# Splitting convolution weights during the seven products, norming the last result by pairs, and moving one stored piece of attention work

## The chip, the cores and the metric

The kernel runs on one core of one Trainium2 chip. Its metric is the device time of one execution in microseconds. Five engines work side by side, each through its own instruction stream in order: PE (TensorE, matrix products), DVE (VectorE), ACT (ScalarE), POOL (GpSimd) and SP (SyncE, which here only issues transfers). ACT also issues transfers, from inside its own stream. An instruction whose inputs or buffers aren't ready blocks everything behind it on its engine.

## The reference, cut to what matters

Two layers on 1024 tokens of width 1024 (all in float32): a windowed grouped-query attention layer, then a Conformer convolution layer, and a last RMSNorm.

```python
proj = h_lat @ w_in                                   # attention layer: q, k, v, z
o = windowed_attention(q, k, v, kc, vc, sink)         # 16 query heads, 4 kv heads, head width 128
y = (o * jax.nn.silu(z)) @ w_out                      # 2048 -> 1024
x = x + gate * y
h = modulate(rmsnorm(x, norm_g[1]), shift, scale)     # convolution layer
a, gl, z = jnp.split(h @ w_in + b_in, 3, axis=-1)     # 1024 -> 3 * 2048
u = a * jax.nn.sigmoid(gl)
u = depthwise_conv_31(u) + dw_b
u = jax.nn.silu(layernorm(u, ln_g, ln_b))
x = x + gate * ((u * jax.nn.silu(z)) @ w_out)         # 2048 -> 1024
return rmsnorm(x, final_g)
```

`depthwise_conv_31` stands for the reference's 31-tap convolution of every channel for itself.

## The kernel before, in words

**Products in float32.** TensorE multiplies in a shorter type, so a float32 operand is *split*: ACT copies it to a rounded high part, and another engine subtracts to get the low part. A product is then three matmuls (high·high, low·high, high·low). For the convolution weights the raw tile is `wraw`, the parts are `whi` (ACT) and `wlo` (DVE or POOL). For the attention output they are `ozf`, `ozh`, `ozl`, and for its weights `wo`, `woh`, `wol`. For the layer's input they are `h2h` (ACT) and `h2l` (DVE), with a helper tile `hf` (ACT) between them.

**Stages in order of time.**

1. Start, modulation vectors, first projections.
2. Attention: 128 steps, `(pr, st)`, a pair of heads and a block of 64 queries each. In a step PE computes scores (`pss`), DVE and ACT make the probabilities, POOL scales them by the row's reciprocal sum (`p_page <- p_page, sc`), and PE transposes them (`pss <- ident, p_page`). Between these PE fills its time with the projection of the next head's weights (`psg`), whose rotary turn is shared by ACT, two transfers issued from ACT's stream, DVE and POOL (`rope_half`), and whose query split is `qh` (ACT) and `ql` (POOL). POOL also prepares sums, differences and low parts of the two output weights in small pieces and stores them in device memory: `low_parts`, a generator of which the step loop takes one piece per step at most, and two in some steps (`wb`, `low`, `lhi`).
3. The attention's output projection by *seven products* in place of eight (`proj_attn`, list `SEQA`): `r = 0` with 8 `kk`, `r = 1..5` with 4 `kk`, each `(r, kk)` 24 matmuls 512 columns wide. The tiles of the next entries are loaded and split ahead by `ahead`. What `split` leaves for DVE (`ozl`) waits in a list until `flush()` is called. `bgA(r, kk)` is called after each entry, for background work. The last three entries (`r = 5`, `kk = 1..3`) are run row block by row block, `b = 0..3`: each block's sum is added to x (`first_sum`, `evac0`), its squares are summed on ACT (`junk`), and `norm0` turns them into a normed row block `xn`. `turn_in` transposes one of eight parts of the normed result on PE into a bank `pso` (two banks take turns) and makes `h2h`, `hf`, `h2l` from it; a bank is free again once `h2l` is made.
4. The convolution layer's input projection: 48 weight tiles (`border`), two halves of the tokens each (`b_mm(i, half)`), 24 matmuls for each. The first `FIRST = 5` tiles run half 0 one after the other, then half 1. Half 1's input is the last result of stage 3, so its eight `turn_in` calls stand inside `b_mm(2..4, 0)` (table `TURNS`), while half 0 only needs earlier results. Behind PE, ACT, DVE and POOL gate (`sig`, `ubuf`) and convolve (`prod`, `odd`, DVE's sums in `pss`).
5. Output projection of the convolution layer, last norm, store.

**What sets the order.** The kernel records operations in the order of the program text, and a planning layer, with a model of the engines, places them into each engine's stream. `tc.high_priority()` moves an operation forward in it, and `after(op, anchor)` ties it behind another one. For `WStream` with `hp=True`, that is the convolution weights, `whi` is made at high priority but tied behind `anchor_n`, the last `xn` written by ACT. Buffers come from two pools: `pg`, 45 pages of 1024 words, and `hp`, 6 half pages of 528. So when a buffer comes free sets when a load may be issued, and SP issues loads strictly in its order.

**Lines touched.** `rstd_one` (one row block's reciprocal root) and its caller `norm0`; `WStream.split`; `proj_attn` around `ahead(*LOAD_TO[i])`, `ahead(10, 9)` and the last block loop; `turn_in`; the step loop's `next(lows, "shut")`; the line that makes `wsB`; `bgA`; the loop over `FIRST`. All engine operations are recorded through one helper, so the profile shows one line number (L94, L96 in the changed kernel) for all of them, and tiles are told apart by name.

## Time and profile before

| | |
|---|---|
| Times of three runs | 1688.74, 1689.21, 1691.45 us, median 1689.21 |
| Profiled execution | 1689.08 us, span 1687.3 us from first to last instruction |
| Mean granted TensorE clock | 0.992 |
| Busy: PE, DVE, ACT, POOL | 1650.8 (98%), 1138.4 (67%), 899.7 (53%), 931.5 (55%) us |
| Start, 0 to 80 us | PE busy 77.0 of 80 us |
| Attention, 80 to 805 us | PE busy 719.8 of 725 us, POOL 457.2 |
| Seven products, 805 to 953 us | PE busy 143.9 of 148 us |
| First convolution tiles, 953 to 1003 us | PE busy 33.6 of 50 us, clock 0.83 |
| Rest of the input projection, 1003 to 1502 us | PE busy 499.0 of 499 us, DVE 473.3, POOL 398.2 |
| Output projection, 1502 to 1679 us | PE busy 177.0 of 177 us |
| Tail | 8.3 us |

How to read it: PE is busy for nearly the whole span, so a change can save time only where PE stands still or its clock is lowered, and it costs time wherever another engine becomes late for PE. The stage table shows where PE stands still. The trace numbers all times from the first instruction of the span.

### The profile page before, as it was taken

The numbers are of one execution on the slowest core, as the hardware profiler recorded it, in microseconds if no ns is written. First come the engines' busy times: TensorE is split into PE (matmuls) and PEld (weight loads), VectorE is DVE, ScalarE is ACT, GpSimd is POOL, SyncE is SP. The second block draws the span as 40 slices with busy tenths as digits, with TensorE's granted clock in tenths as the row PEclk, the third lists the DMA queues.
The fourth block names the chain that finished last, engine by engine and source line by source line (L and its number), as shares of the span: only waits on it lengthen the run. The fifth ranks groups of instructions, "written<-read, shape, count | busy, mean of one in ns | idle before, by whom it ended". The sixth has DMA issues, their size and how long they took to land.

```text
span 1687.3 us, 23985 instructions
## 1 busy us (share of the span) xinstructions
PE 1650.8 (98%) x8244; PEld 1379.1 (82%) x8244; DVE 1138.4 (67%) x2089; ACT 899.7 (53%) x1573; POOL 931.5 (55%) x877
## 2 busy tenths in 40 slices
PE   9999999999999999999999879999999999999998
PEld 6888888888888888888788658888888888888886
DVE  5755544555354554556477789999999998868722
ACT  6644543555355544556228486555656554566831
POOL 0338774686458674772110089999889887130400
PEclk9999999999999999999999989999999999999999
DMA  9435553564356653577778412020211202377971
GB/s 383 167 92 165 157 171 94 166 194 143 96 166 194 197 156 117 170 226 254 273 268 327 152 50 89 13 75 13 76 50 51 82 34 80 130 269 249 320 285 50
DMA packets 151321, 263.53 MB, mean 156 GB/s; under 512 B 46122, under 2 KB 62818, under 8 KB 151200
## 3 DMA queue, kind: packets, MB, share of 16 engines
q1 hardware_dynamic: 142816, 247.84, 43.9%
q10 hardware_dynamic: 8384, 14.16, 2.9%
q8 instruction: 65, 1.06, 0.3%
q14 instruction: 56, 0.46, 0.1%
HBM read 197.19 MB, written 54.27 MB: 149 GB/s over the span
## 4 chain that ended last, share of the span: by engine, by line
PE 85%; DMA 4%; POOL 3%; DVE 3%; ACT 2%; issue 2%; ACTq 0%; SPq 0%; POOLq 0%; DVEq 0%
PE psg L94 45%; PE pso L94 21%; PE pss L94 19%; DMA rope_half<-rope_half 2%; POOL rope_half L94 1%; DVE x_page L94 1%; POOL lhi_half L94 1%; DMA wraw_page<-in_k_win_dram 1%; POOL wlo_page L94 1%; DMA wo_page<-wslow 0%; POOL ql_page L94 0%; DMA araw_page<-in_k_ada_dram 0%; POOL p_page L94 0%; ACT whi_page L94 0%; DVE pss L94 0%
## 5 line engine op out<-in xcount | busy, mean ns | idle before, releaser
L94 POOL TENSOR_TENSOR odd_half<-odd_half,prod_half 128x513 f32<-128x513 f32 (+2 forms) x252 | 317.0, 1264 | 17.7 <-ACT prod_half L94 3.7
L94 PE MATMUL psg<-hh_page,whi_page 128*128 128x512 f32 x600 | 236.8, 395 | 0.0
L94 PE MATMUL psg<-hl_page,whi_page 128*128 128x512 f32 x600 | 234.8, 391 | 0.0
L94 PE MATMUL psg<-hh_page,wlo_page 128*128 128x512 f32 x600 | 234.3, 391 | 0.0
L94 ACT ACTIVATE prod_half<-ubuf,dww 128x513 f32<-128x513 f32 (+2 forms) x252 | 164.9, 674 | 124.8 <-POOL odd_half L94 118.6
L94 POOL TENSOR_TENSOR wlo_page<-wraw_page,whi_page 128x512 fp32r<-128x512 f32 (+1 forms) x104 | 170.8, 1659 | 107.5 <-ACT whi_page L94 103.9
L94 PE MATMUL psg<-h2h_page,whi_page 128*128 128x512 f32 x464 | 183.0, 394 | 11.1 <-ACT whi_page L94 11.1
L94 PE MATMUL psg<-h2h_page,wlo_page 128*128 128x512 f32 x464 | 181.5, 391 | 4.5 <-POOL wlo_page L94 4.5
L94 PE MATMUL psg<-h2l_page,whi_page 128*128 128x512 f32 x464 | 181.3, 391 | 0.0
L94 DVE SCALAR_TENSOR_TENSOR pss<-ubuf,wsum,pss 128x512 f32<-128x512 f32 (+3 forms) x270 | 174.2, 674 | 1.4
L94 DVE SCALAR_TENSOR_TENSOR pss<-ubuf,dww,pss 128x512 f32<-128x512 f32 (+3 forms) x270 | 173.9, 674 | 1.4
L94 ACT ACTIVATE pt<-pss 128x640 fp32r<-128x640 f32 (+1 forms) x128 | 86.5, 676 | 140.3 <-PE pss L94 127.8
L94 POOL TENSOR_SCALAR p_page<-p_page,sc 128x576 f32<-128x576 f32 (+2 forms) x128 | 93.2, 729 | 98.2 <-DVE sc L94 94.0
L94 DVE CUSTOM_DVE_ANT_0 p_page<-pss,mask_page,nsink 128x576 f32<-128x576 f32 (+1 forms) x112 | 90.2, 805 | 75.9 <-PE pss L94 57.3
L94 ACT ACTIVATE p_page<-p_page,sc 128x577 f32<-128x577 f32 (+2 forms) x128 | 96.9, 757 | 68.0 <-DVE sc L94 66.0
L94 PEld LDWEIGHTS psg<-hh_page,wlo_page 128*128 128x128 f32 x600 | 112.7, 188 | 24.4 <-POOL wlo_page L94 0.3
L94 DVE TENSOR_TENSOR pt<-pss,pt 128x640 fp32r<-128x640 f32 (+1 forms) x128 | 100.7, 787 | 44.2 <-ACT pt L94 43.9
L94 PEld LDWEIGHTS psg<-hh_page,whi_page 128*128 128x128 f32 x600 | 112.8, 188 | 19.7 <-ACT hh_page L94 0.3
L94 PEld LDWEIGHTS psg<-hl_page,whi_page 128*128 128x128 f32 x600 | 113.1, 188 | 19.1 <-DVE hl_page L94 0.2
L94 PE MATMUL pso<-h2h_page,whi_page 128*128 128x512 f32 x304 | 118.3, 389 | 0.0
L94 PE MATMUL pso<-h2l_page,whi_page 128*128 128x512 f32 x304 | 118.3, 389 | 0.0
L94 PE MATMUL pso<-h2h_page,wlo_page 128*128 128x512 f32 x304 | 118.3, 389 | 0.0
(294 smaller groups left out, 3980.6 us busy)
## 6 DMA issues: line engine op xcount, KB each, us to landing
wraw_page<-in_k_wconv_dram SPq DMA_DIRECT2D x48, 512.0 KB, 3.3
wraw_page<-in_k_win_dram SPq DMA_DIRECT2D x40, 512.0 KB, 4.2
wo_page<-in_conv_w_out_dram SPq DMA_DIRECT2D x32, 512.0 KB, 5.7
wol_page<-wolC SPq DMA_DIRECT2D x32, 512.0 KB, 5.9
ozf_page<-ozd SPq DMA_DIRECT2D x28, 512.0 KB, 7.1
rope_half<-rope_half ACTq DMA_DIRECT2D x76, 128.0 KB, 3.2
araw_page<-in_k_ada_dram SPq DMA_DIRECT2D x16, 512.0 KB, 10.0
dww_raw<-in_ada_w_dram SPq DMA_DIRECT2D x64, 128.0 KB, 2.4
```

The lines of the kernel that those rows point to most:

```text
L94: r = f(*a, **k)
```

## The change

1. **Weight tiles of stage 4 are loaded and split earlier.** A table `AHEAD_B` names, for entries `(r, kk)` of the seven products, when `bgA` loads and splits: loads at (1,3), (2,1), (2,3), (3,2) and two at (5,2); splits at (2,1), (2,3), (3,1), (5,2). Before, two loads stood at (4,3), and splits at (5,0) and (5,2). The loop over `FIRST` no longer splits in its first turn. The low parts of tiles 0 and 1 go to POOL in place of DVE, and for tiles 0 to 3 in two halves.
2. **`flush()` is called after two more `ahead` calls.**
3. **The last result is normed by pairs of row blocks.** `rstd_one` is gone; `norm0` runs for blocks 0 and 1 together and for 2 and 3 together, with `rstd_of` on two columns. In the last block loop the DVE part of the two `turn_in` calls (`h2l`) is held back until `first_sum` and `evac0` of the block are recorded.
4. **`hf` is a half page (`hp`) in place of a page (`pg`)**, and the pages `sig` and `zsb` are allocated after the seven products.
5. **In attention** each group of 32 steps takes no piece of `low_parts` at step 13 and two at step 20. Before, both took one.

```diff
+AHEAD_B = {(1, 3): ("load",), (2, 1): ("split", "load"), (2, 3): ("split", "load"), (3, 1): ("split",), (3, 2): ("load",),
+           (5, 2): ("split", "load", "load")}
...
-    def rstd_one(ssum, n, part):
-
-        ms, sq, r, q = (small([P, 1], name=k) for k in ("ms1", "sq1", "rr1", "rq1"))
-        V.tensor_scalar(out=ms, in0=ssum, scalar1=1.0 / n, scalar2=part, op0=ALU.mult, op1=ALU.add)
-        act(sq, ms, AF.Sqrt)
-        V.reciprocal(r, sq)
...
                     after(act(h, r, AF.Copy), anchor_n)
-                    split_lo(self.lo_eng(i), l, r, h)
+                    for a in range(0, KT, KT // 2 if i < 4 else KT):
+                        sl = slice(a, a + (KT // 2 if i < 4 else KT))
+                        split_lo(self.lo_eng(i), *(t[:, sl] for t in (l, r, h)))
...
                 ahead(*LOAD_TO[i])
+                flush()
...
         ahead(10, 9)
+        flush()
...
-                        if b < 2:
-                            later.popleft()()
+                        low = later.popleft()(True) if b < 2 else None
                         first_sum(1, 0, b, acc[b], part("m", b), True)
                         evac0(1, 0, b, xr, acc[b])
-                        norm0(1, 0, b)
+                        if low:
+                            low()
+                        if b % 2:
+                            norm0(1, 0, (b - 1, b + 1))
...
-    def norm0(h, m, at=None):
+    def norm0(h, m, span=(0, 4)):
...
-        if at is None:
-            r = rstd_of(ss[1], D, 4, ss[0])
-            rows = [(b, r[:, b:b + 1]) for b in range(4)]
-        else:
-            rows = [(at, rstd_one(ss[1][:, at:at + 1], D, ss[0][:, at:at + 1]))]
+        b0, b1 = span
+        r = rstd_of(ss[1][:, b0:b1], D, b1 - b0, ss[0][:, b0:b1])
+        rows = [(b, r[:, b - b0:b - b0 + 1]) for b in range(b0, b1)]
...
-        f = pg.alloc(F32, [1024], "hf")
+        f = hp.alloc(F32, None, "hf")
...
-            stt(H2l[(h, kt)], tv, mod1[:, 8 + kt:9 + kt], fv, ALU.mult, ALU.subtract)
-        pg.free(f)
+
+        def low():
+            with tc.high_priority():
+                stt(H2l[(h, kt)], tv, mod1[:, 8 + kt:9 + kt], fv, ALU.mult, ALU.subtract)
+            hp.free(f)
...
+        if hold:
+            return low
+        low()
...
-            lstate[0] = next(lows, "shut")
-            if qb == 3 and h % 4 < 3:
+            for _ in range({13: 0, 20: 2}.get(i % 32, 2 if qb == 3 and h % 4 < 3 else 1)):
                 lstate[0] = next(lows, "shut")
...
-    wsB = WStream(hp=True, lo_eng=lambda i: V if i < 2 or i % 3 == 0 and i > 3 else G, srcs=[...])
+    wsB = WStream(hp=True, lo_eng=lambda i: V if i % 3 == 0 and i > 3 else G, srcs=[...])
...
     def bgA(r, kk):
-        if (r, kk) == (4, 3):
-            wsB.load()
-            wsB.load()
-        if r == 5:
-            if kk != 1:
-                wsB.split()
+        for what in AHEAD_B.get((r, kk), ()):
+            getattr(wsB, what)()
...
         b_mm(i, 0)
         wsB.load()
-        wsB.split()
+        if i:
+            wsB.split()
         wsB.load()
```

**In the built program** PE's stream is the same, instruction by instruction. The other streams are ordered anew by the planner in the places that the change touches. Three places are shown here, each before and in the changed kernel.

ACT at the join of stages 3 and 4, from the last `xn` of the norm on. First before; `whi_page_9623` is tile 2's, the one that PE needs next:

```order
L94 ACTIVATE xn_page_9556<-x_page_9316,r_619_9591 128x512
L94 ACT_TABLE_LOAD
L94 ACTIVATE sig_page_8375<-psg_9595,vt 128x512
L94 ACTIVATE whi_page_9848<-wraw_page_9693 128x1024
L94 ACTIVATE whi_page_9771<-wraw_page_9687 128x1024
L94 ACTIVATE whi_page_9623<-wraw_page_9621 128x1024
L94 ACTIVATE odd_half_9656<-ubuf,vt,dww 128x249
```

ACT at the same place now; the three `whi` are those of tiles 6, 5 and 7:

```order
L96 ACTIVATE xn_page_9587<-x_page_9337,r_609_9583 128x512 x2
L96 ACT_TABLE_LOAD
L96 ACTIVATE sig_page_9591<-psg_9593,vt 128x512
L96 ACTIVATE whi_page_9836<-wraw_page_9681 128x1024
L96 ACTIVATE whi_page_9759<-wraw_page_9437 128x1024
L96 ACTIVATE whi_page_9908<-wraw_page_9763 128x1024
L96 ACTIVATE odd_half_9646<-ubuf,vt,dww 128x249
```

Five `prod` follow as before, and then these rows, of which the first is the split of tile 4:

```order
L96 ACTIVATE whi_page_9677<-wraw_page_9435 128x1024
L96 ACTIVATE h2h_page_9693<-pso_9695,mod_611 128x512
L96 ACTIVATE whi_page_10132<-wraw_page_9840 128x1024
L96 ACTIVATE h2h_page_9693<-pso_9723,mod_611 128x512
L96 ACTIVATE sig_page_9591<-psg_9683,vt 128x512
L96 ACTIVATE hf_half_9700<-h2h_page_9693,bcol 128x512
```

The splits of tiles 0 to 3 now stand ahead of the norm's end. The first `hf` of half 1 stands behind the `sig` of tile 2 (`psg_9683`).

POOL in attention, the third group of 32 steps, around step 15 (whose probabilities are the 448-wide `p_page`; `lhi` is the piece of `low_parts`). First before:

```order
L94 TENSOR_TENSOR wlo_page_5509<-wraw_page_5065,whi_page_5508 128x512 x2
L94 TENSOR_TENSOR lhi_half_5534<-low_page_5409,lhi_half_5534 128x512
L94 TENSOR_TENSOR ql_page_5379<-rope_half_5497,qh_page_5378 128x8x64
L94 TENSOR_SCALAR p_page_5549<-p_page_5549,sc_5550 128x448
L94 TENSOR_TENSOR lhi_half_5576<-low_page_5409,lhi_half_5576 128x512
```

POOL at the same place now:

```order
L96 TENSOR_TENSOR wlo_page_5509<-wraw_page_5065,whi_page_5508 128x512 x2
L96 TENSOR_TENSOR ql_page_5379<-rope_half_5497,qh_page_5378 128x8x64
L96 MEMSET p_page_5543 128x64
L96 TENSOR_TENSOR rope_half_5596<-rope_half_5596,sin_page_567 128x512
L96 TENSOR_SCALAR p_page_5543<-p_page_5543,sc_5544 128x448
L96 TENSOR_TENSOR lhi_half_5570<-low_page_5409,lhi_half_5570 128x512
```

The piece `lhi` has left the place ahead of `ql`, and a rotary product has come in ahead of `p_page`. In the first and the fourth group the piece has left the place ahead of `ql` as well, and `p_page` stands right behind `ql`. On ACT, in the third group, the two transfers that this product waits for now stand like this, and `p_page_5543<-nsink` between them waits for POOL's `wlo_page_5509`:

```order
L96 ACTIVATE whi_page_5609<-wraw_page_5161 128x1024
L96 DMA rope_half_5596<-rope_half_5595 64x512
L96 ACTIVATE p_page_5543<-nsink 128x1
L96 DMA rope_half_5596<-rope_half_5595 64x512
L96 ACTIVATE p_page_5543,sc_5544<-p_page_5543,sc_5544 128x449
```

SP, the loads for `r = 5` of the seven products. The tiles `ozf` of `kk = 0, 1, 2, 3` are numbered 9081, 9087, 9178, 9220. First before:

```order
L94 DMA ozf_page_9081<-ozd 128x2x512
L94 DMA ozf_page_9087<-ozd 128x2x512
L94 DMA ozf_page_9178<-ozd 128x2x512
L94 DMA wo_page_9182<-wslow 128x1024
L94 DMA wo_page_9180<-wsums 128x1024
L94 DMA xr_page_9190<-in_x_dram 128x512 x2
L94 DMA xr_page_9191<-in_x_dram 128x512 x2
L94 DMA ozf_page_9220<-ozd 128x2x512
```

SP at the same place now, where they are 9102 (some rows ahead of these), 9108, 9199 and 9241; `wraw_page_9066` is a load of a convolution weight:

```order
L96 DMA wraw_page_9066<-in_k_wconv_dram 128x1024
L96 DMA wo_page_9112<-wslow 128x1024
L96 DMA ozf_page_9108<-ozd 128x2x512
L96 DMA wo_page_9110<-wsums 128x1024
L96 DMA wo_page_9106<-wslow 128x1024
L96 DMA xr_page_9212<-in_x_dram 128x512
L96 DMA xr_page_9211<-in_x_dram 128x512 x2
L96 DMA xr_page_9212<-in_x_dram 128x512
L96 DMA ozf_page_9241<-ozd 128x2x512
L96 DMA wo_page_9243<-wsums 128x1024
L96 DMA ozf_page_9199<-ozd 128x2x512
```

The load of `kk = 2`, which stood right behind that of `kk = 1`, now stands behind the residual's loads (`xr`) and behind the load of `kk = 3` and its weights. The latter two reuse pages of which ACT's stream still writes x to device memory (`x1d`), and wait for these writes to land. On ACT, `ozh` of `kk = 2` stands ahead of the first `h2h` of stage 3's `turn_in` calls, as before.

More of the change, by code (lines that the diff above doesn't have):

```diff
@@ L215, in rstd_end @@
         return r2
-    def rstd_one(ssum, n, part):
-        ms, sq, r, q = (small([P, 1], name=k) for k in ("ms1", "sq1", "rr1", "rq1"))
-        V.tensor_scalar(out=ms, in0=ssum, scalar1=1.0 / n, scalar2=part, op0=ALU.mult, op1=ALU.add)
-        act(sq, ms, AF.Sqrt)
-        V.reciprocal(r, sq)
-        V.tensor_scalar(out=q, in0=r, scalar1=r, scalar2=-0.5, op0=ALU.mult, op1=ALU.mult)
-        V.tensor_scalar(out=q, in0=q, scalar1=ms, scalar2=1.5, op0=ALU.mult, op1=ALU.add)
-        out = small([P, 1], name="r21")
-        V.tensor_scalar(out=out, in0=q, scalar1=r, scalar2=None, op0=ALU.mult)
-        return out
     def mm3(o, wh, wl, rh, rl, start, stop):
@@ L1106, in norm0, with turn_in @@
             for kt in range(KT):
-                later.append(lambda h=h, kt=kt: turn_in(h, kt))
-    def turn_in(h, kt):
+                later.append(lambda hold=False, h=h, kt=kt: turn_in(h, kt, hold))
+    def turn_in(h, kt, hold=False):
         if kt % 2 == 0:
@@ L1629, in backbone_kernel @@
     boff = {"a": 0, "gl": 16, "z": 32}
-    wsB = WStream(hp=True, lo_eng=lambda i: V if i < 2 or i % 3 == 0 and i > 3 else G, srcs=[k_wconv[off[k] // P + j] for k, j in border])
+    wsB = WStream(hp=True, lo_eng=lambda i: V if i % 3 == 0 and i > 3 else G, srcs=[k_wconv[off[k] // P + j] for k, j in border])
     zsd = dr.tile([NJ, P, T], F32, tag="zsd", name="zsd")
@@ L1856, in backbone_kernel @@
     held_at = []
-    sigp = pg.alloc(F32, [2, 512], "sig")
-    zsp = pg.alloc(F32, [2, 512], "zsb")
     yready, spilled = set(), set()
-    zbuf = [zsp]
+    zbuf = []
     def b_mm(i, half):
@@ L2131, in backbone_kernel @@
     pg.free(*gbc0)
+    sigp = pg.alloc(F32, [2, 512], "sig")
+    zbuf.append(pg.alloc(F32, [2, 512], "zsb"))
     for i in range(FIRST):
```

## The prediction

> **What bounds the kernel now.** I read the page first, then the waits of PE, then the windows around the largest waits. The page says that PE is the bound.
>
> ```profile
> PE 1650.8 (98%) x8244; PEld 1379.1 (82%) x8244; DVE 1138.4 (67%) x2089; ACT 899.7 (53%) x1573; POOL 931.5 (55%) x877
> ```
>
> The span is 1687.3 us, so PE stands still for some 36 us in all, and a gain has to come from there or from its clock. The waits of PE (who is waited for: us in total, times, longest) name the places:
>
> ```profile
> PE psg L94 <- ACT whi_page L94: 11.1, 1, 11.1
> PE pss L94 <- POOL p_page L94: 5.1, 4, 1.7
> ...
> PE pso L94 <- DVE ozl_page L94: 3.7, 1, 3.7
> ...
> PE pso L94 <- DVE h2l_page L94: 0.8, 2, 0.4
> ```
>
> The first, and a wait of 4.46 us that follows it, are the join between the seven products and the convolution layer. Of the windows (busy time of PE, PEld, DVE, ACT, POOL with counts, then the granted clock) the first row lies right behind these waits, at half clock; the second is the rest of the input projection:
>
> ```profile
> 980.00:985.00 5.00, 3.68 (x10) 2.93 (x11) 4.64 (x11) 0.54 (x2) 4.93 (x4) 0.50 0.00 0
> 1003.00:1502.00 499.00, 499.00 (x2210) 413.09 (x2209) 473.33 (x747) 289.37 (x411) 398.20 (x288) 1.00 0.22 73
> ```
>
> From 1003 us on PE never waits (499.0 of 499 us, 0.226 us for each of 2210 matmuls), so what the join saves is lost again only if another engine becomes late there.
>
> **The join: what is removed.** PE's own rows (start, us, idle before):
>
> ```profile
> 975.64 0.79 PE L94 MATMUL psg<-h2h_page,whi_page 128*128 128x512 f32 x1 [11.12 <-ACT whi_page L94]
> 981.32 0.80 PE L94 MATMUL psg<-h2h_page,wlo_page 128*128 128x512 f32 x1 [4.46 <-POOL wlo_page L94]
> ...
> 985.71 0.39 PE L94 MATMUL psg<-h2l_page,whi_page 128*128 128x512 f32 x1
> ```
>
> PE stops at 975.64 - 11.12 = 964.5. From 975.64 to the row at 985.71 there are ten matmuls, 2.3 us at the 0.226 us of the window above, and one set of four transposes, some 0.4 us. Without any wait the row at 985.71 would start at 964.5 + 2.7 = 967.2, so the two waits and the half clock behind them cost 18.5 us. With the two short waits for `h2l` (0.8 us) 19.3 us can go. Why it waits stands on ACT:
>
> ```profile
> 970.03 0.72 ACT L94 ACTIVATE xn_page<-x_page,r 128x512 f32<-128x512 f32 x1 [0.98 <-DVE r L94]
> 970.77 1.28 ACT L94 ACT_TABLE_LOAD   x1
> 972.07 0.69 ACT L94 ACTIVATE sig_page<-psg,vt 128x512 f32<-128x512 f32 x1
> 972.65 2.94 ACT L94 ACTIVATE whi_page<-wraw_page 128x1024 fp32r<-128x1024 f32 x3
> ```
>
> The split of tile 2 comes after the last `xn`, as the third of three `whi`, and POOL's `wlo` of tile 2 as the third of its three. In the changed kernel tiles 0 to 3 are split during the seven products, so both waits lose their cause. Their four `whi` (0.98 us each) now land on ACT in that stage, the one in the busiest place ahead of this row:
>
> ```profile
> 909.80 1.06 ACT L94 ACTIVATE ozh_page<-ozf_page 128x1024 fp32r<-128x1024 f32 x1 [2.30 <-DMA ozf_page<-ozd]
> ```
>
> ACT waits 2.3 us for a load there, which takes up 1 us more of work. I cost the splits at nothing, and at 1 us if that cover is gone.
>
> **The join: what is added.** The norm of half 1 ends earlier. DVE's chain per row block takes 4.76 us (963.84 to 968.60 below); in pairs it is some 7.3 us for two (six adds of 0.7, one wait of 0.8 for `junk`, one chain of 1.4, two `xn` of 0.4). That is 2.2 us for each pair; two `wlo` of 1.23 us go from DVE, and the order of `h2l` gives the rest. Worked through row by row, the last `xn` on ACT ends at 960.8 instead of 970.75.
>
> ```profile
> 963.84 0.21 DVE L94 TENSOR_SCALAR ms<-ssx,ssx 128x1 f32<-128x1 f32 x1 [0.79 <-ACT junk_half L94]
> 968.60 0.21 DVE L94 TENSOR_SCALAR ms<-ssx,ssx 128x1 f32<-128x1 f32 x1 [0.79 <-ACT junk_half L94]
> 941.19 1.23 DVE L94 TENSOR_TENSOR wlo_page<-wraw_page,whi_page 128x1024 fp32r<-128x1024 f32 x1 [0.20 <-ACT whi_page L94]
> ```
>
> What is late next are the `turn_in` calls inside tile 2. PE ends tile 1 at 964.5 and tile 2 with two sets of transposes at 971.0; the third set needs the first one's bank, which `h2l` frees. On ACT: table and `sig` to 962.8, three `whi` to 965.7, `odd` (which needs `ubuf`, 965.8) to 966.3, five `prod` (2.06 us) to 968.4, `whi`, `h2h`, `whi`, `h2h` to 971.7, and `sig` of tile 2, which stands ahead of `hf`, to 972.4. Then `hf` to 973.1 and DVE's `h2l` to 973.8: a wait of 2.8 us. The next `hf` takes a half page that POOL's `odd` gives back: two `wlo` to 969.2, `ubuf` and `odd` to 970.6, `wlo` to 972.9, three `odd` (0.8 us) to 975.3; `hf` ends at 976.4, `h2l` at 977.2, PE wants the bank at 976.5: 0.8 us more. The durations:
>
> ```profile
> 975.98 2.06 ACT L94 ACTIVATE prod_half<-ubuf,dww 128x249 f32<-128x249 f32 x5
> 974.28 6.98 POOL L94 TENSOR_TENSOR wlo_page<-wraw_page,whi_page 128x1024 fp32r<-128x1024 f32 x3
> 984.21 10.37 POOL L94 TENSOR_TENSOR odd_half<-odd_half,prod_half 128x249 f32<-128x249 f32 x13
> 987.38 0.75 DVE L94 SCALAR_TENSOR_TENSOR h2l_page<-pso,mod,hf_page 128x512 fp32r<-128x512 f32 x1 [1.12 <-ACT hf_page L94]
> ```
>
> So 19.3 - 3.6 = 15.7 us. Does the clock fall in a wait of 2.8 us? The trace has a wait of 1.68 us without a fall (window 729:734, clock 1.00) and one of 3.74 us with one:
>
> ```profile
> 731.05 0.66 PE L94 MATMUL pss<-ident,p_page 128*128 128x128 f32 x4 [1.68 <-POOL p_page L94]
> 729.00:734.00 5.00, 3.32 (x20) 2.66 (x19) 2.04 (x5) 1.30 (x4) 5.00 (x7) 1.00 0.73 248
> 838.95 0.79 PE L94 MATMUL pso<-woh_page,ozl_page 128*128 128x512 f32 x1 [3.74 <-DVE ozl_page L94]
> 842.42 0.40 PE L94 MATMUL pso<-wol_page,ozh_page 128*128 128x512 f32 x1
> ```
>
> After the latter eight matmuls took 3.47 us (838.95 to 842.42) in place of 1.82: a fall costs 1.65 us. 2.8 is nearer to 3.74 than to 1.68, so I count it: **the join gives 14.0 us**, between 10 (the last `xn` only at 965, so everything behind it 4 us later) and 19.3 (no new wait).
>
> **Step 13 to step 20.** The wait for `p_page` in step 15 falls in three of four groups:
>
> ```profile
> 167.39 0.66 PE L94 MATMUL pss<-ident,p_page 128*128 128x128 f32 x4 [0.59 <-POOL p_page L94]
> 541.83 0.66 PE L94 MATMUL pss<-ident,p_page 128*128 128x128 f32 x4 [1.46 <-POOL p_page L94]
> ...
> 536.10 2.56 POOL L94 TENSOR_TENSOR wlo_page<-wraw_page,whi_page 128x512 fp32r<-128x512 f32 x2
> 538.61 1.31 POOL L94 TENSOR_TENSOR lhi_half<-low_page,lhi_half 128x512 f32<-128x512 f32 x1
> 539.87 1.28 POOL L94 TENSOR_TENSOR ql_page<-rope_half,qh_page 128x512 fp32r<-128x512 f32 x1
> 541.13 0.64 POOL L94 TENSOR_SCALAR p_page<-p_page,sc 128x448 f32<-128x448 f32 x1
> ```
>
> POOL runs without a break, so taking out the piece (1.31 us, 1.26 from start to start) brings `p_page` forward by that. In the first group 0.59 us go, in the fourth 1.26 of 1.68. In the third the planner has put a rotary product ahead of `p_page`, and its second transfer is issued by ACT only when POOL's `wlo` is done, at 538.6. How long such a transfer takes to be seen by POOL:
>
> ```profile
> 528.02 1.12 ACTq L94 DMA_DIRECT2D rope_half<-rope_half  x2
> 531.51 1.30 POOL L94 TENSOR_TENSOR rope_half<-rope_half,sin_page 128x512 f32<-128x512 f32 x1 [2.71 <-DMA rope_half<-rope_half]
> ```
>
> The second of that pair starts at about 528.5, so 3.0 us. Then the product runs from 541.7 to 543.0 and `p_page` to 543.7, 1.9 us later than before. The wait of PE becomes 3.4 us, near the 3.74 that lowered the clock: another 1.65. So 0.6 + 1.3 - 3.6 = **-1.7 us**, between +3.1 (the product's transfers are early) and -4. At step 20, seven steps of some 5.6 us later, I cost the second piece at nothing: POOL is idle for 268 of the stage's 725 us (table above), a third of each step, which covers 1.3 us. It costs up to 1.3 us in each group if that cover is gone.
>
> **The loads of r = 5.** Here the change costs something. SP issues `ozf` of `kk = 2` behind loads that wait for writes of x. The rows of ACT, its writes, and what stands behind:
>
> ```profile
> 909.91 1.37 ACTq L94 DMA_DIRECT2D x1d<-x_page  x2
> 920.78 1.04 ACT L94 ACTIVATE ozh_page<-ozf_page 128x1024 fp32r<-128x1024 f32 x1
> 922.67 0.76 ACT L94 ACTIVATE h2h_page<-pso,mod 128x512 fp32r<-128x512 f32 x1
> 925.62 0.60 PE L94 MATMUL pso<-ident,xn_page 128*128 128x128 f32 x4
> DMA to landing us min/median/max: 5.8/6.9/7.0
> DMA to landing us min/median/max: 6.9/6.9/6.9
> ```
>
> The last two rows are the writes of x (905 to 916 us) and an `ozf` load (from 917 us). The second write is issued near 910 and lands at 917; `ozf` goes out at about 917.3 and lands at 924.1, where before `ozh` ran at 920.78. ACT stands still, and behind this `ozh` and its `woh` stands the `h2h` of the first `turn_in`: `ozh`, `woh`, `h2h`, `hf` take 3.3 us, `h2l` 0.8, so the bank is free at 928.2, and PE wants it at 925.62 (third set of transposes): 2.6 us. DVE's sums behind it add some 0.4. **-3.0 us**, between 0 (the transfer lands in 3 us once the queues are emptier) and -6.
>
> **Sum.** 14.0 - 1.7 - 3.0 = 9.3 us from the profiled 1689.1 us (span and 1.8 us around it): **1679.8 us**. That execution lies 0.1 us under the median of the three, so nothing is corrected for it.
>
> The Trainium skill ("TensorE: Matmul & The Clock Gate", part 1, "What's actually happening") states that the clock falls after an idle window of about 3.4 us, a window that runs freely. By that rule waits of 2.8 and 3.4 us would not lower it; the fall after 3.74 us agrees with it, and no wait between 1.7 and 3.7 us is in this trace.
>
> **The rivals.**
>
> - *The clock stays up* in the two new waits: 2 x 1.65 us less, 1676.5 us. For it speaks that 1.68 us left it alone. The rule above is this one.
> - *The new waits don't come*: bank, rotary product and `ozf` are in time. Then 19.3 + 3.1 us go, 1666.7 us, and with one of the three waits left about 1670. For it: the transfers of the trace also land in 2.8 us at best. Against it: the waits follow from the order within the streams.
> - *The convolution stage keeps the gain.* DVE's first `ubuf` comes at 965 in place of 972.78, only 7.8 us earlier, while PE is 15.7 ahead, and DVE is busy 473 of 499 us. If it had no slack, 8 us would come back as waits of PE for DVE: 1687.8; with half of it 1683.8. Against it: 26 us of idle time, and PE never waits for it before.
> - *Slower*: the late `ozf` decides. Without that term the change gives 12.3 us, so to become 0.2% slower (3.4 us) it must cost 15.7 us: `ozf` would have to go out 12.7 us later than 917.3, at 930, which needs writes of x that take 20 us. With 20 us of cost the time is 1696.8. That a write of x takes 6.9 us speaks for full queues and some delay; the longest, 7.0 us, against so much.
> - *It doesn't do what it says*: the early splits are held up by loads that come late, tile 2 again waits for the norm, and only the norm's gain is left. With the costs above that is about 1689. The loads go out some 40 us ahead of their use, which speaks against it.
>
> **How the numbers follow.** Forecast 0.42 (own range 1677.5 to 1683), clock stays up 0.18, new waits don't come 0.14, convolution stage 0.14, slower 0.07, not as it says 0.05. 0.2% (3.4 us) is about what can be told from no change. Below 1685.7 lie the first three and half of the fourth: 0.81. Within 0.2%: the rest of the fourth and most of the last, 0.11. Slower: 0.08. The range, 1669.5 to 1687.5, cuts off part of the third case at the low end and the two last cases, about 0.2 in all.
>
> **What would show each step.** Right: no wait of PE for `whi` or `wlo` near 965; a wait for `h2l` of about 2.8 us at tile 2's end; a wait for `p_page` of about 3.4 us near 541 and none at 167; a wait of PE for `h2l` near 925, with ACT waiting for `ozf`. Wrong: PE waiting for DVE between 1003 and 1500, or a new wait elsewhere in the seven products, or a total under 1670 with none of the new waits.

## The result, and the profile after

The changed kernel takes 1677.84 us (median of 4 runs, 1676.32 to 1679.51), the kernel before beside it 1690.07 us (1688.74 to 1691.45): a ratio of 0.9928, 95% interval 0.9911 to 0.9945, or 12.2 us less. The forecast was 1679.8 us. The profiled execution of the change is the slowest of its four, 1679.51 us with a span of 1677.7 us, 9.6 us under the profiled one of before. The waits of PE in it (who is waited for: us in total, times, longest):

```profile
PE pso L96 <- DVE h2l_page L96: 5.1, 3, 2.2
PE pss L96 <- POOL p_page L96: 4.9, 3, 2.9
...
PE pss L96 <- DVE sc L96: 1.9, 1, 1.9
PE pso L96 <- POOL wol_page L96: 1.2, 1, 1.2
PE psg L96 <- DVE ozl_page L96: 1.1, 1, 1.1
PE psg L96 <- ACT woh_page L96: 0.7, 1, 0.7
```

The waits for `whi` and `wlo` of the join (11.1 and 4.5 us) and the wait of 3.7 us for `ozl` at 839 us are gone. Longer are the waits for `h2l` (5.1 us, 0.8 before). New are waits for `sc`, `wol` and `woh`, and one for `ozl` at another place (899 us).

PE executes the same 8244 matmuls in the same order in both kernels and in all kernels below. So the start of one matmul in one trace can be taken from its start in the other, and the growth of that difference over a stretch is what the stretch costs. All rows are against the profiled execution of before, in us, minus is a gain; half-clock windows lie inside the numbers. A group is one of the four groups of 32 attention steps; group 2 changes by 0.1 us at most and is left out, and so is the start up to 80 us, where the profiles differ by -0.6 to +1.2 us. "Halves" counts windows of 3.41 us at half clock outside the last 10 us (before: 6, five of them at the join). The medians are those of the runs.

| kernel | median | group 1 | group 3 | group 4 | `ozl` at 839 | r = 1 | r = 2, 3 | r = 4, 5 | join | tile 2 to 1003 | halves |
|---|---|---|---|---|---|---|---|---|---|---|---|
| the change | 1677.84 | -0.6 | +7.4 | -1.7 | -5.6 | +1.6 | +2.4 | +2.8 | -18.3 | +1.9 | 2 |
| step_only | 1691.85 | -1.0 | +4.9 | -1.5 | +1.1 | 0.0 | 0.0 | 0.0 | 0.0 | -0.7 | 8 |
| no_step | 1676.70 | +0.2 | +0.7 | -0.8 | -5.6 | +1.6 | +2.7 | +4.8 | -18.3 | +1.9 | 1 |
| step_not_g3 | 1672.91 | -1.0 | 0.0 | -2.4 | -5.6 | +1.6 | +2.4 | +3.3 | -18.3 | +2.3 | 2 |
| flush_only | 1686.15 | -0.2 | +0.5 | -0.4 | -5.6 | +1.7 | 0.0 | 0.0 | -0.1 | 0.0 | 5 |
| no_flush | 1681.30 | -0.3 | +7.3 | -1.6 | 0.0 | 0.0 | +2.4 | +3.6 | -18.3 | +2.4 | 5 |
| late_splits | 1679.94 | -0.6 | +4.9 | -1.8 | -5.6 | +1.6 | 0.0 | 0.0 | -12.6 | +4.1 | 4 |
| splits_later | 1677.09 | -1.1 | +4.5 | -1.3 | -5.6 | +1.6 | +1.9 | +2.6 | -18.3 | +1.9 | 1 |
| xr_later | 1676.48 | -0.8 | +4.5 | -1.9 | -5.6 | +1.6 | +2.4 | +1.4 | -18.3 | +2.4 | 2 |
| norm_rows | 1680.97 | -0.9 | +4.6 | -1.0 | -5.6 | +1.6 | +2.4 | +5.0 | -16.9 | +3.3 | 4 |
| low_plain | 1683.64 | -0.3 | +4.9 | -1.8 | -5.6 | +1.6 | +2.4 | +2.8 | -15.3 | +4.5 | 2 |
| join_undone | 1681.79 | -0.4 | +4.8 | -2.1 | -5.6 | +1.6 | 0.0 | 0.0 | -7.1 | +1.0 | 3 |
| best | 1669.98 | -1.0 | +0.4 | -2.1 | -5.6 | +1.6 | 0.0 | +3.3 | -18.3 | +2.2 | 1 |

From 1011 us to 1600 us no kernel gains or loses against before by more than 0.02 us (only low_plain has a last wait for `h2l` just ahead of that): the convolution stage took nothing back. The kernels are told below.

### The profile page after: what moved, and what is told of

Read it like the earlier page. It is cut to its first block, busy times and chain, and to the rows that moved or that the text cites. A ratio compares the mean times of both kernels' runs of the same rounds, so it can differ in the third digit from the quotient of the medians.

```text
span 1677.7 us, 23953 instructions
## 1 busy us (share of the span) xinstructions
PE 1650.4 (98%) x8244; PEld 1378.2 (82%) x8244; DVE 1131.1 (67%) x2077; ACT 901.5 (54%) x1571; POOL 933.3 (56%) x883
## 4 chain that ended last, share of the span: by engine, by line
PE 88%; issue 3%; DMA 3%; DVE 2%; POOL 2%; ACT 1%; SPq 0%; ACTq 0%; POOLq 0%; DVEq 0%
PE psg L96 46%; PE pso L96 22%; PE pss L96 20%; DMA rope_half<-rope_half 1%; DVE x_page L96 1%; POOL rope_half L96 1%; DMA araw_page<-in_k_ada_dram 1%; POOL wlo_page L96 1%; DVE ozl_page L96 0%; POOL lhi_half L96 0%; DMA wo_page<-wsums 0%; DVE part_page L96 0%; DMA xr_page<-in_x_dram 0%; ACT ozh_page L96 0%; SPq L96 0%
## 5 line engine op out<-in xcount | busy, mean ns | idle before, releaser
L96 POOL TENSOR_TENSOR odd_half<-odd_half,prod_half 128x513 f32<-128x513 f32 (+2 forms) x252 | 312.6, 1248 | 31.0 <-ACT prod_half L96 18.0
L96 POOL TENSOR_TENSOR wlo_page<-wraw_page,whi_page 128x512 fp32r<-128x512 f32 (+1 forms) x110 | 179.0, 1644 | 214.2 <-ACT whi_page L96 144.9
L96 PEld LDWEIGHTS psg<-hl_page,whi_page 128*128 128x128 f32 x600 | 113.5, 189 | 19.3 <-DVE hl_page L96 0.2
```

The source lines that it names most:

```text
L96: r = f(*a, **k)
```

## The experiments

### The piece at step 13

Alone on the kernel before:

```diff
-            lstate[0] = next(lows, "shut")
-            if qb == 3 and h % 4 < 3:
+            for _ in range({13: 0, 20: 2}.get(i % 32, 2 if qb == 3 and h % 4 < 3 else 1)):
                 lstate[0] = next(lows, "shut")
```

> The kernel before with the move of the piece alone. Theory: 1690.07 + 5.05 = 1695.1 us, the wait for ozl of 3.74 us near 839 stays, since the product before it moves with PE. Rival 1, the prediction's size: 1691.8 us. Rival 2, the 3.74 us wait for ozl is tied to transfers and swallows the delay: about 1690 us and a wait for ozl that is nearly gone.

Measured: 1691.85 us, ratio 1.0009 (1.0 to 1.0018). The other way round, the change without this edit (no_step):

> The change with the stored piece left at step 13. Theory: in the third attention group the missing piece shifts the pages, the 448-column softmax gets the page of a raw weight tile and waits for POOL's wlo (PE waits 1.95 us for sc, then 2.93 us for p_page, then 6.8 us of half clock, 7.45 us in all), while groups 1 and 4 win 0.74 and 1.66 us; the move costs 5.05 us, so this kernel takes 1677.84 - 5.05 = 1672.8 us, and its PE waits at 541 only 1.5 us for p_page. Rival 1, the prediction's own size: the move costs 1.7 us, 1676.1 us. Rival 2, what attention loses is won back by later waits that are tied to transfers: 1677.8 us.

Measured: 1676.70 us, ratio to before 0.9919 (0.9905 to 0.9934). And the change with the piece moved in three groups of four:

```diff
-            for _ in range({13: 0, 20: 2}.get(i % 32, 2 if qb == 3 and h % 4 < 3 else 1)):
+            for _ in range(({} if i // 32 == 2 else {13: 0, 20: 2}).get(i % 32, 2 if qb == 3 and h % 4 < 3 else 1)):
```

> The change with the piece moved in groups 1, 2 and 4 only. Theory: group 3 alone costs 7.45 us, so 1677.84 - 7.45 = 1670.4 us; the waits at 167 and 731 stay gone, the one at 541 is 1.5 us. Rival 1, the prediction's size of group 3 (3.6 us): 1674.2 us. Rival 2, the loss moves on to the group that now holds a different number of pieces at its start: 1677 us or more, with a new wait in group 4.

Measured: 1672.91 us, ratio to before 0.9896 (0.9881 to 0.9911), 4.9 us under the change.

The sign and the place hold: group 3 loses, groups 1 and 4 win. The size that I had read from the one profile of the change, 5.05 us in all, falls in all three. Of the nine profiles with the move in group 3 seven lose 4.5 to 4.9 us there, and two lose 7.4 and 7.3. With the common 4.8, less 0.8 and 1.6 of the other two groups, the move costs 2.4 us; the runs say 1.7 (step_only) and 1.1 (no_step), where the wait at r = 5 happened to be 1.5 us longer. What happens in group 3, first PE and POOL of the change, then DVE and ACT:

```profile
539.09 0.36 PE L96 MATMUL pss<-kh_page,qh_page 128*128 128x192 f32 x1 [1.95 <-DVE sc L96]
...
538.24 1.30 POOL L96 TENSOR_TENSOR ql_page<-rope_half,qh_page 128x512 fp32r<-128x512 f32 x1
...
543.81 1.26 POOL L96 TENSOR_TENSOR rope_half<-rope_half,sin_page 128x512 f32<-128x512 f32 x1 [4.17 <-DMA rope_half<-rope_half]
545.05 0.64 POOL L96 TENSOR_SCALAR p_page<-p_page,sc 128x448 f32<-128x448 f32 x1
...
538.34 0.68 DVE L96 CUSTOM_DVE_ANT_1 p_page<-pss,mask_page,nsink 128x448 f32<-128x448 f32 x1 [0.69 <-POOL wlo_page L96]
...
538.35 0.47 ACTq L96 DMA_DIRECT2D rope_half<-rope_half  x1
```

There are two waits, not one. The rotary product stands ahead of `p_page`, as predicted, and waits for a transfer issued at 538.35 us. It is there 5.5 us later, not 3.0 us. The move did not make it slow. The forecast had taken its 3.0 us from a pair issued 10 us earlier, while the pair at this place (the first issued at 538.12 us) took 6.2 us to land in the trace of before too:

```profile
538.12 0.47 ACTq L94 DMA_DIRECT2D rope_half<-rope_half  x1
DMA to landing us min/median/max: 6.2/6.2/6.2
```

What makes one pair slow and the other fast is not shown: in before the DMA engines were 0.85 busy around the fast one (528 to 531.5 us) and 0.83 around the slow one (538.2 to 541.6 us). The other wait comes earlier. DVE's softmax of 448 columns runs at 538.34 us where it ran at 533.84 us: with one piece less the pages fall out differently, and it now gets the page of a raw weight tile, so that it waits for POOL's `wlo` to have read that. PE waits 1.95 us for its `sc`. That page was not in the forecast.

The two waits, 4.9 us, stand where before one of 1.46 us stood. Why two profiles lose 7.4 us stands in the windows of the change (length, busy time of PE, PEld, DVE, ACT, POOL with counts, granted clock, DMA share, GB/s), cut at the places where the clock changes:

```profile
538.20:541.60 3.40, 2.51 (x14) 2.20 (x15) 2.94 (x8) 2.66 (x7) 1.44 (x3) 1.00 0.90 234
541.60:545.00 3.40, 1.21 (x6) 0.66 (x4) 0.16 (x1) 0.00 (x0) 1.19 (x1) 1.00 0.38 103
545.00:548.40 3.40, 2.66 (x12) 2.57 (x13) 0.88 (x2) 1.11 (x2) 3.40 (x5) 0.50 0.15 9
548.40:551.90 3.50, 3.50 (x10) 2.73 (x9) 0.21 (x1) 0.63 (x1) 3.50 (x4) 0.51 0.74 253
```

The clock is set from window to window: a window in which PE worked 1.21 of 3.4 us was followed by one at half clock, which was itself not full and was followed by another. In the change this came in the wait for `p_page`: of the 7.4 us, 4.0 are more waiting than before and 3.0 go to the two windows at half clock. In step_only the grid lay 1.1 us earlier, the first wait brought one window of half clock, and PE, slower, then waited only 1.3 us for `p_page`: 2.8 us of waiting and 1.7 of half clock, 4.9 us in all. In join_undone it is 4.4 us of waiting and no half clock, 4.8 us in all. So the seven profiles agree in the sum, not in its parts. All nine also have a wait of 0.4 us for `p_page` near 588 us, worth 0.7 us, which the kernels without the move in group 3 don't have. It stands behind the second piece of step 20, which the forecast had costed at nothing; its chain was not followed further.

### The flush calls

```diff
                 ahead(*LOAD_TO[i])
-                flush()
...
         ahead(10, 9)
-        flush()
```

> The change without the two added flush calls, so that DVE has the four sums of x again ahead of the second and third ozl. Theory: the wait of PE for ozl (3.7 us) and the half clock behind it (1.65 us) come back, 1677.84 + 5.4 = 1683.2 us. Rival, the prediction's silence on these calls: they cost and give nothing, 1677.8 us; the wait for ozl was swallowed by the delay of attention.

Measured: 1681.30 us, ratio to before 0.9943 (0.9926 to 0.9959), 3.5 us above the change. And the two calls alone on the kernel before:

> The kernel before with the two added flush calls alone. Theory: the 3.74 us wait for ozl and the 1.65 us of half clock behind it go, a wait of 1.2 us for wol behind it stays or comes: 1690.5 - 4.2 = 1686.3 us. Rival 1, the prediction's silence on them: 1690.5 us. Rival 2: without the wait PE meets the late POOL wol and ozf of the next row and loses all of it there: 1690 us with a wait of 4 us near 845.

Measured: 1686.15 us, ratio 0.9978 (0.9968 to 0.9987), 3.7 us less than before. The theory for flush_only is met (1686.3 us). For no_flush it asked for 5.4 us and got 3.5, because it left out what comes back behind: in both pairs 5.6 us go at `ozl` and 1.6 us come back. DVE of before, then of the change, then PE of no_flush and of the change:

```profile
830.72 0.69 DVE L94 TENSOR_TENSOR x_page<-psg,part_page 128x512 f32<-128x512 f32 x1 [4.63 <-PE psg L94]
...
837.67 4.58 DVE L94 TENSOR_TENSOR ozl_page<-ozf_page,ozh_page 128x1024 fp32r<-128x1024 f32 x3
```

```profile
832.80 1.23 DVE L96 TENSOR_TENSOR ozl_page<-ozf_page,ozh_page 128x1024 fp32r<-128x1024 f32 x1 [1.13 <-ACT ozh_page L96]
836.31 0.69 DVE L96 TENSOR_TENSOR x_page<-psg,part_page 128x512 f32<-128x512 f32 x1 [2.28 <-PE psg L96]
```

```profile
844.82 0.50 PE L96 MATMUL pso<-woh_page,ozl_page 128*128 128x512 f32 x1 [3.73 <-DVE ozl_page L96]
```

```profile
847.98 0.50 PE L96 MATMUL pso<-wol_page,ozh_page 128*128 128x512 f32 x1 [1.24 <-POOL wol_page L96]
```

Without the call DVE stands in its queue before the sums of x, which wait for PE, and the `ozl` that PE needs next is behind them. With it the `ozl` comes first, and PE waits 7 us later for POOL's `wol`, 1.24 us.

### The early splits

Loads and splits at their old places, with the rest of the change:

```diff
-AHEAD_B = {(1, 3): ("load",), (2, 1): ("split", "load"), (2, 3): ("split", "load"), (3, 1): ("split",), (3, 2): ("load",),
-           (5, 2): ("split", "load", "load")}
+AHEAD_B = {(4, 3): ("load", "load"), (5, 0): ("split",), (5, 2): ("split",)}
...
-        if i:
-            wsB.split()
+        wsB.split()
```

> The change with the loads and splits of the first convolution weights at their old places (two loads at the end of r = 4, two splits in r = 5, the rest after the products); the norm by pairs, the held h2l and the flush calls stay. Theory: the norm by pairs alone brings the last xn 10 us forward, so that of the 11.1 us for whi 1 to 2 are left and the 4.5 us for wlo stay: 6 us and one or two windows of half clock at the join, in place of 3.4 us of waits for h2l. The waits near 889, 895 and 925 (0.8, 1.3 and 2.7 us), which come from the early splits and their loads, go. Sum within 2 us of the change, 1677.8. Rival: only the early splits free the join; then whi and wlo wait 13 to 15 us as before, 1685 to 1690 us.

Measured: 1679.94 us, ratio to before 0.9939 (0.9924 to 0.9954), 2.1 us above the change, about the 2 us of the theory. The waits for `whi` and `wlo` are smaller than it had them (3.5 for 6 us), but one for `h2l` stays at tile 2's end, where it had none:

```profile
964.30 0.50 PE L95 MATMUL psg<-h2h_page,whi_page 128*128 128x512 f32 x1 [1.51 <-ACT whi_page L95]
967.03 0.79 PE L95 MATMUL psg<-h2h_page,wlo_page 128*128 128x512 f32 x1 [2.00 <-POOL wlo_page L95]
981.44 0.66 PE L95 MATMUL pso<-ident,xn_page 128*128 128x128 f32 x4 [3.19 <-DVE h2l_page L95]
```

So the early splits bring the join 8.0 us (18.3 - 1.9 against 12.6 - 4.1) and cost 2.4 us at r = 2 and 3 and 2.8 us at r = 4 and 5, which are 0.0 here. Why they cost anything at r = 2 and 3 is seen on POOL, DVE, ACT and PE of the change:

```profile
879.65 2.90 POOL L96 TENSOR_TENSOR wlo_page<-wraw_page,whi_page 128x512 fp32r<-128x512 f32 x2 [22.35 <-ACT whi_page L96]
892.76 3.23 POOL L96 TENSOR_TENSOR wlo_page<-wraw_page,whi_page 128x512 fp32r<-128x512 f32 x2 [10.20 <-issue]
...
881.35 2.29 DVE L96 TENSOR_TENSOR ozl_page<-ozf_page,ozh_page 128x1024 fp32r<-128x1024 f32 x1 [1.21 <-ACT ozh_page L96]
890.76 1.23 DVE L96 TENSOR_TENSOR ozl_page<-ozf_page,ozh_page 128x1024 fp32r<-128x1024 f32 x1 [1.21 <-ACT ozh_page L96]
893.05 1.78 DVE L96 TENSOR_TENSOR x_page<-x_page,gate_page 128x512 f32<-128x512 f32 x1
896.45 0.68 DVE L96 TENSOR_TENSOR x_page<-x_page,gate_page 128x512 f32<-128x512 f32 x1
...
889.67 1.06 ACT L96 ACTIVATE ozh_page<-ozf_page 128x1024 fp32r<-128x1024 f32 x1 [7.41 <-DVE ozf_page L96]
...
891.73 0.50 PE L96 MATMUL psg<-woh_page,ozh_page 128*128 128x512 f32 x1 [0.67 <-ACT woh_page L96]
899.05 0.50 PE L96 MATMUL psg<-woh_page,ozl_page 128*128 128x512 f32 x1 [1.13 <-DVE ozl_page L96]
```

The same subtraction takes DVE 1.23 us alone and 2.29 us while POOL works on `wlo`, the half one 0.68 and 1.78 us; DVE's sums `x_page<-psg,part_page`, with an operand in PSUM, keep their 0.68 us beside POOL. From 881.35 to 889.56 us DVE works without a break, and ACT's `ozh`, and the `woh` behind it that PE waits for, come only after DVE's `ozf`; the second stretch makes `ozl` itself late. The Trainium skill ("GPSIMD Engine Reference", section "Specifications") states that GpSimd shares its SBUF interfaces with VectorE, and that they contend in instructions with two SBUF inputs; the rows agree, to the operand (2.29 us for 1.23 with two SBUF inputs, 0.68 unchanged with one of them in PSUM). To see whether these stretches make the waits, the second and third split were moved:

```diff
-AHEAD_B = {(1, 3): ("load",), (2, 1): ("split", "load"), (2, 3): ("split", "load"), (3, 1): ("split",), (3, 2): ("load",),
+AHEAD_B = {(1, 3): ("load",), (2, 1): ("split", "load"), (2, 3): ("load",), (3, 0): ("split",), (3, 2): ("load",), (3, 3): ("split",),
```

> The change with the second and third early split moved from the ends of rows (2,3) and (3,1) to (3,0) and (3,3), where DVE works on operands that lie in PSUM or is idle. Theory: POOL's wlo stretches a DVE subtraction with both operands in SBUF from 1.22 to 2.3 us (0.69 to 1.78 for the half size), which makes woh and ozl late for PE near 889 and 895; moved, DVE's operations take 1.22 us there and the waits of 0.8 and 1.3 us go: 1675.7 us. Rival: these waits come from the transfers or the order on ACT: they stay, 1677.8 us, though DVE is no longer stretched there.

Measured: 1677.09 us, ratio to before 0.992 (0.9905 to 0.9935): 0.8 us under the change, less than the spread of its runs. In the trace the `wlo` at 879.65 us is that of row (2,1), which I had left, so the first stretch stayed with its wait (0.6 us). The sums of the second stretch take 0.69 us again and its wait of 1.1 us is gone, but POOL now runs beside another pair of sums, these take 1.78 and 1.67 us, and PE waits 0.6 us one row on. The run times alone tell neither theory from the rival; that the late operations moved along with POOL's work speaks for the theory. The best version below moves the first split as well, and both waits are gone there; it moves loads too, so it does not prove the point by itself.

### The loads of r = 5

```diff
-            if kk == 1 and r in (3, 4, 5):
+            if kk == (3 if r == 4 else 1) and r in (3, 4, 5):
                 xr = residual(*{3: (0, 1), 4: (1, 1), 5: (1, 0)}[r])
```

> The change with the loads of the residual for the sum of r = 4 issued two rows later, so that the last two ozf loads stand ahead of them in SP's queue. Theory, the prediction's term for r = 5: ozf goes out before the writes of x have landed, ACT does not wait for it, and the waits of PE for h2l near 925 (2.15 and 0.55 us) go: 1677.84 - 2.7 = 1675.1 us. Rival: ozf lands late because the queues are full, or its page is freed late, wherever it stands: 1677.8 us with the wait still there.

Measured: 1676.48 us, ratio to before 0.992 (0.9906 to 0.9935), 1.4 us under the change, where 2.7 us were expected; that is within the spread of its runs (1675.84 to 1680.04), but the traces show the same 1.4 us at this place. SP and ACT of the change, then of xr_later, each with PE's wait:

```profile
915.06 2.61 SPq L96 DMA_DIRECT2D xr_page<-in_x_dram  x4
919.12 0.38 SPq L96 DMA_DIRECT2D ozf_page<-ozd  x1
920.69 0.37 SPq L96 DMA_DIRECT2D ozf_page<-ozd  x1
...
927.28 1.06 ACT L96 ACTIVATE ozh_page<-ozf_page 128x1024 fp32r<-128x1024 f32 x1 [1.86 <-DMA ozf_page<-ozd]
...
931.84 0.66 PE L96 MATMUL pso<-ident,xn_page 128*128 128x128 f32 x4 [1.99 <-DVE h2l_page L96]
```

```profile
916.84 0.37 SPq L96 DMA_DIRECT2D ozf_page<-ozd  x1
...
923.49 1.06 ACT L96 ACTIVATE ozh_page<-ozf_page 128x1024 fp32r<-128x1024 f32 x1 [0.51 <-DMA ozf_page<-ozd]
...
928.05 0.66 PE L96 MATMUL pso<-ident,xn_page 128*128 128x128 f32 x4 [0.66 <-DVE h2l_page L96]
```

The cause is as predicted: with `xr` behind it, `ozf` goes out 3.9 us earlier in the trace (PE itself is 2.5 us earlier there) and PE waits 0.66 us in place of 1.99. It is not all: ACT still waits half a microsecond for `ozf`, and 1.4 of the 2.8 us stay.

### What the join is made of

The norm row by row, all else as in the change:

```diff
-                        if b % 2:
-                            norm0(1, 0, (b - 1, b + 1))
+                        norm0(1, 0, b)
```

> The change with the norm of the last result row by row as before; the early splits stay. Theory: the norm is the later of the two, so the last xn comes 8 to 10 us later and the waits of PE for h2l at the end of tile 2 grow from 3.4 to about 11 us, with two or three windows of half clock: 1685 to 1690 us. Rival: the early splits alone free the join, since PE has tiles 0 to 2 to work on meanwhile: 1677.8 us.

Measured: 1680.97 us, ratio to before 0.9941 (0.9924 to 0.9957), 3.1 us above the change. Both theories miss: in before's time the last `xn` ends at 963.5 us in place of 960.2, so 3.3 us later and not 8 to 10, and the norm counts for 2.8 us of the 16.4 at the join. With the splits late as well:

> The change without both of its parts at the join: splits and loads at their old places and the norm row by row. Splits late alone cost 2.1 us (1679.94), norm by rows alone 3.1 us (1680.97). Theory: each part alone hides most of what the other would leave, so both undone cost far more than the sum: the waits for whi and wlo (11.1 and 4.5 us) and the half clock come back, less the 4.3 us of waits near 889, 895 and 925 that go: 1687 to 1690 us. Rival: the two add up, 1683 us.

Measured: 1681.79 us, ratio to before 0.9952 (0.9937 to 0.9966). The theory falls; the rival's sum, 1683 us, was the near one. The table says why: at the join the splits bring 8.0 us and the norm 2.8, and both undone cost 10.3 (16.4 - 6.1), so they add up. And 6.1 us of gain are still there with neither, which points to the rest of the edit. (That the low parts of tiles 0 and 1 went to POOL, in halves, was not tried alone.) The last kernel of this group takes back the h2l that is held behind the sums, and gives `hf` a full page again (the two were not tried apart):

```diff
-        f = hp.alloc(F32, None, "hf")
+        f = pg.alloc(F32, [1024], "hf")
...
-                        low = later.popleft()(True) if b < 2 else None
+                        low = later.popleft()() if b < 2 else None
```

> The change with hf in a full page again and the h2l of the last block not held back behind the sums. Theory: these two parts only order DVE and pages around the first transposes; held, the sums of x come 0.75 us earlier in two blocks, so without it the norm ends up to 1.5 us later and PE waits that much more for h2l at the end of tile 2: 1677.8 to 1679.3 us. Rival: hf from the shared pages delays another page's owner as before, 1681 us or more.

Measured: 1683.64 us, ratio to before 0.9963 (0.9951 to 0.9976), 5.8 us above the change; in the profiles 3.0 at the join and 2.6 behind it. The time is the rival's, the place is the theory's: the last `xn` ends at 965.1 us in before's time, 4.9 us later. DVE of low_plain, and of the change:

```profile
951.19 0.75 DVE L96 SCALAR_TENSOR_TENSOR h2l_page<-pso,mod,hf_page 128x512 fp32r<-128x512 f32 x1 [2.20 <-ACT hf_page L96]
956.28 0.75 DVE L96 SCALAR_TENSOR_TENSOR h2l_page<-pso,mod,hf_page 128x512 fp32r<-128x512 f32 x1 [2.21 <-ACT hf_page L96]
```

```profile
953.68 0.75 DVE L96 SCALAR_TENSOR_TENSOR h2l_page<-pso,mod,hf_half 128x512 fp32r<-128x512 f32 x1 [0.20 <-ACT hf_half L96]
956.41 0.74 DVE L96 SCALAR_TENSOR_TENSOR h2l_page<-pso,mod,hf_half 128x512 fp32r<-128x512 f32 x1
```

I had counted the 0.75 us of the operation that is held back. What it holds up is the wait in front of it: DVE stands 2.2 us for ACT's `hf`, twice, with the sums that feed the norm behind. Held, the sums fill that time. How much of the 5.6 us belongs to this and how much to the full page stays open.

### The parts that cost, taken out

```diff
-AHEAD_B = {(1, 3): ("load",), (2, 1): ("split", "load"), (2, 3): ("split", "load"), (3, 1): ("split",), (3, 2): ("load",),
+AHEAD_B = {(1, 3): ("load",), (2, 2): ("split", "load"), (3, 1): ("split", "load"), (3, 3): ("split", "load"),
            (5, 2): ("split", "load", "load")}
...
-            if kk == 1 and r in (3, 4, 5):
+            if kk == (3 if r == 4 else 1) and r in (3, 4, 5):
...
-            for _ in range({13: 0, 20: 2}.get(i % 32, 2 if qb == 3 and h % 4 < 3 else 1)):
+            for _ in range(({} if i // 32 == 2 else {13: 0, 20: 2}).get(i % 32, 2 if qb == 3 and h % 4 < 3 else 1)):
```

> The change with the piece moved in groups 1, 2 and 4 only, the residual of r = 4 loaded two rows later, and the early splits at rows (2,2), (3,1), (3,3) and (5,2). Theory: the gains add up. 1672.9 us (measured without group 3's move), less 2.2 us of waits near 895 and 889, less 1.4 us near 925, and a fall of the clock less: 1668 to 1670 us, with no wait of PE for woh, ozl or h2l over 0.7 us between 880 and 930. Rival: PE then arrives earlier at the join and waits there for h2l by as much more: 1672 to 1673 us.

Measured: 1669.98 us, ratio to before 0.9882 (0.9868 to 0.9897), 7.9 us under the change, at the upper end of the theory. PE's waits:

```profile
PE pso L96 <- DVE h2l_page L96: 3.1, 2, 2.2
PE pss L96 <- POOL p_page L96: 2.7, 2, 1.4
...
PE pso L96 <- POOL wol_page L96: 1.2, 1, 1.2
PE pso L96 <- DVE xn_page L96: 0.7, 1, 0.7
```

The waits for `woh` and `ozl` are gone, r = 2 and 3 cost 0.0 us, and the join keeps its 18.3 us. What is left there is one wait of 2.2 us for `h2l`. The gains do not quite add up, though: r = 4 and 5 cost 3.3 us, more than the 2.8 of the change. The wait there for `h2l` has shrunk to 0.8 us, but 1.7 us are new ahead of it. ACT waits for the load of a weight, the norm behind it comes late, and PE's four transposes follow the row blocks of `xn` one by one, 0.4 us apart in place of 0.1. ACT and PE of best:

```profile
908.07 1.07 ACT L96 ACTIVATE woh_page<-wo_page 128x1024 fp32r<-128x1024 f32 x1 [3.78 <-DMA wo_page<-wsums]
...
913.39 1.52 PE L96 MATMUL pso<-ident,xn_page 128*128 128x128 f32 x4 [0.67 <-DVE xn_page L96]
```

Which of the moved loads and splits makes that weight late was not tried.

## Why the prediction was right, point by point

The time, 1677.84 us, lies 2 us under the forecast and well inside the range. The sum came out by more than its own steps, though.

- **The join, removed 19.3 us:** right. 18.3 us go up to the end of the half clock, and the two short waits for `h2l` behind it (0.4 and 0.4 us) go too.
- **The join, the last `xn`:** right in time. In the change it ends at 967.0 us, where PE is 6.8 us late from the stages before, so at 960.2 us in before's time; 960.8 was forecast. The parts were weighed less well: row by row (norm_rows) it ends 3.3 us later, where the two pairs stood for 4.4 us, and with `h2l` not held and `hf` in a full page (low_plain) 4.9 us later, where some 3 us were left for the order of `h2l`.
- **The join, the new waits of 2.8 and 0.8 us:** there, as 2.24 and 0.88 us for `h2l`. The step that failed is "a fall costs 1.65 us. 2.8 is nearer to 3.74 than to 1.68, so I count it". The clock does not go by the length of a wait (last section): in the change it stayed up here, which is half of a rival that had 0.18; in the other wait, for `p_page` near 541 us, it fell as forecast, for two windows and not one. (That the trace of before has no wait between 1.7 and 3.7 us was misread as well: PE waits 2.0 us for `zerr_page` at the very start. It says nothing of the clock, which is on record only from 6 us on.) And where it fell at this place, as in xr_later and best, the stretch cost only 0.4 us more (+2.3 against +1.9 in the table), since PE, slower, did not wait the second time. The join gave 16.4 us, not 14.0.
- **The early splits, "at nothing, and at 1 us if that cover is gone":** wrong. They cost 2.4 us, and not on ACT, where I looked, but through DVE, which POOL's part of the split slows. This is the term that the forecast put at nothing.
- **Step 13 to 20, -1.7 us:** right in size (1.1 to 1.7 us by the runs, 2.4 by most profiles), in the sign of each group and in the rotary product. In group 3 the forecast had 3.6 us, and 4.8 is the common loss. Missing were the page that makes DVE's softmax late (PE waits 1.95 us), the transfer's 5.5 us against 3.0, which the row at its own place would have given (6.2 us), and the 0.7 us behind step 20.
- **The loads of r = 5, -3.0 us:** right: 2.8 us in the change, by the mechanism given; 2.6 to 5.0 us in the other profiles with these loads and the same order, the larger ones with a window of half clock. xr_later shows half of it to be the order on SP.
- **Not in the prediction at all:** the two flush calls. I quoted their wait, 3.74 us for `ozl`, and the half clock behind it, as evidence for the clock, and never asked what it waited for. They give 3.7 us.
- **The convolution stage keeps the gain:** it did not happen, no PE wait for DVE between 1003 and 1500 us. Slower by the late `ozf`: neither; the load went out at 920.69 us with PE 4.1 us late, so at 916.6 us in before's time, where 917.3 was the sum's.

With the usual values of the stretches the change is -16.4 at the join, +2.4 for the step, +2.8 at r = 4 and 5, +2.4 at r = 2 and 3 and -4.0 for the flush calls, -12.8 us; the runs say -12.2. The forecast had -14.0, +1.7, +3.0 and two zeros, -9.3 us. That the time was met to 2 us is in part luck: the two terms that were not seen, +2.4 and -4.0, have opposite signs, and the gain was missed by 2.9 us, of which 1.0 does not show in the time because the kernel before ran at 1690.07 us beside the change, not at the 1689.1 us that the forecast started from.

## What to carry to other kernels

For each line of a diff that only changes when something is emitted, look up which wait in the profile stands behind the place it is emitted at; the two calls that looked like housekeeping were worth a third of the gain. When work goes to an idle engine, look for what the neighbour does at that moment with operands in the same memory: "idle" is no price of zero. An operation that waits in an in-order queue costs what it waits, not what it takes. And take the time of a transfer from the row at its own place: a transfer of the same size took 3.0 us to be seen at one place and 6.2 us to land at another, 10 us on.
